# Retention norm: sums by a constant stationary operand, and the factor spread by transfers

## The chip, the cores and the metric

The kernel is one layer of a hybrid encoder on one core of a Trainium2 chip. The metric is the device time of one execution in microseconds (us). A profiled execution gives a trace of every instruction, and a page that sums it up. The engines are TensorE (PE in the rows; its weight loads are PEld), VectorE (DVE), ScalarE (ACT), GpSimd (POOL) and SyncE (SP), which here issues the transfers. SPq in a row is a transfer that SyncE's queue issues.

## The reference

One layer has a combined input projection, eight retention heads and eight windowed attention heads side by side, an output projection, a layer norm, a SwiGLU feed-forward block and a second layer norm. What the change touches is the group norm of the retention heads. Each head has 64 channels, and each position is normalized over them:

```
y = y_f + y_b
mu = jnp.mean(y, axis=-1, keepdims=True)
var = jnp.mean(jnp.square(y - mu), axis=-1, keepdims=True)
y = (y - mu) * lax.rsqrt(var + GN_EPS)
y = ... * gn_gain                       # per channel
return y * jax.nn.silu(gate)
```

Sequence length is 1024, model width 1024, and everything is float32.

## The kernel before, in words

The span has these stages: the first projections (0 to 64 us), the attention of the first pair of heads with more projections (to 120), four retention pairs, each but the first together with an attention pair (to 344), a tail, and from 357.6 on the output projection and the feed-forward block.

**Layout.** A retention pair is two heads. Their output y is held as 128 partitions (2 heads x 64 channels) by 1024 positions, in two halves of 512. The mean is already zero, since the values are centred when they are projected. So the norm needs, for each head and position, the sum of squares over 64 partitions, and the factor (sum / 64 + eps) to the power −1/2 on each of those 64 partitions.

**The norm of a half** has four steps in the class `Retention`. `out` (line 476) makes a 128x512 bank of PSUM called bo. `evict` lets ScalarE write the squares to the buffer rb (line 483) and VectorE copy y (line 484). `norm` has TensorE take each 128x128 block of squares as the stationary operand, with two columns of a constant moving through it (line 490, four matmuls in the code and eight in the trace). The sums come out with positions on the partitions, 128x8. VectorE scales them (line 492), GpSimd raises them to the power −1/2 (line 493), and ScalarE copies each number 64 times (line 495). `turn` has TensorE transpose the four blocks back (line 500), and VectorE multiplies y by the gain and by the factor out of PSUM (line 502).

**Order.** TensorE's order is written out by hand: `run` takes a list of steps in which F stands for a share of the fillers, that is, steps of the remaining projections (`mm3`: three 128x512 matmuls, lines 77 to 79). In the list, K is the keys (transposes, line 404, and VectorE's key evictions, line 407), Y is `out`, E `evict`, M `norm`, X `turn`, Q the retention scores; `sco`, `trn` and `val` are the attention's steps. A pair's second norm and second turn, M(1) and X(1), stand in the list of the next pair, and those of the last pair in a short tail. The other engines' orders are set by a scheduler. Every filler step counts one tick, 48 in a pair's list and 16 in the tail, and the lists `later` and `side` release work when a tick is reached.

**Presplit.** The work in `side` prepares operands for later products: `put` (lines 581 to 584) splits a matrix into a high part (ScalarE, line 582) and a low part (VectorE, line 583) and stores both to DRAM by SyncE (line 584): to pgd and ptd, to wod for the output projection and to ped for a later product. In the last pair, all splits use one buffer called aq. After the last stores SyncE loads the first product's operands from wod (line 794, buffers w and u in turn). TensorE starts the product at lines 783 to 785, and its first sum takes four such operands, w, u, w, u. The transfers of the scan's states stand at line 443, and a small start load with 64 partitions by 8 numbers at line 203.

Of the kernel before, what the change touches and what calls it, by code (L numbers as in the profile page):

```python
# [30 lines left out]
LAG = 3  # L31
NLAG = 7


C_ID, C_DP, C_DN = 0, 128, 256
C_QD, C_BASE = 384, 512
C_KF, C_KB, C_MH, C_TWO, C_BD = 896, 897, 898, 899, 900
C_W = 902

C_MF, C_MB = 902, 1030  # L40


def layer(tc, xT, xn, w_first, w_mt, w_rv, w_out, w_pg, w_pe, pT, w_gu, w_dn,
# [148 lines left out]
    mraw = bt([P, 2, P], "sq", 1)  # L192
    sp.dma_start(mraw, consts[:, C_MF:C_MF + 2 * P].rearrange("p (a b) -> p a b", a=2))
    pool.tensor_copy(masks, mraw)
# [5 lines left out]
    rr = cp.tile([P, 24], F32, name="rr")  # L200
# [3 lines left out]
    lt = cp.tile([P, 4, 24], F32, name="lt")  # L204
# [11 lines left out]
    dve.scalar_tensor_tensor(lg, rr, -1.0, t_, ALU.mult, ALU.mult)  # L216
    kd = cp.tile([P, 2, 8], F32, name="kd")
# [119 lines left out]
    def proj_rv():  # L337
# [12 lines left out]
        def step(t, kt):  # L350
# [5 lines left out]
            if kt == KT - 1:  # L356
                g = b.rearrange("p (g e) -> p g e", e=64)
                sm = bt([P, 3, 8], "sm", 2)
                dve.tensor_reduce(sm[:, 0, :], g, AX.X, ALU.add, negate=True)
                dve.scalar_tensor_tensor(rv[:, t, :].rearrange("p (g e) -> p g e", e=64),  # L360
                                         sm[:, 0, :].unsqueeze(2).to_broadcast([P, 8, 64]), 1.0 / 64, g,
                                         ALU.mult, ALU.add)
# [25 lines left out]
    class Retention:  # L388


        def __init__(self, i, y, states):
            self.i, self.y, self.states = i, y, states
            self.rk, self.dq, _ = pairs[i]
            self.U = [bt([P, NT - 1, 64], f"kv{d}") for d in range(2)]
            self.kdec, self.pt, self.qq, self.r = {}, {}, {}, {}
# [17 lines left out]
        def kv(self):  # L413

            for q in range(2):
# [64 lines left out]
        def evict(self, hh):  # L480
            of = self.o.rearrange("p n c -> p (n c)")
            sq = self.sq = bt([P, HF], "rb")
            act.activation(sq, of, AF.Square)
            dve.tensor_copy(self.half(hh), of)

        def norm(self, hh):

            b = self.o[:, :, 0:2]
            for j in range(4):
                pe.matmul(b[:, j, :], self.sq[:, j * P:(j + 1) * P], cst[:, C_BD:C_BD + 2], start=True, stop=True)  # L490
            sm = bt([P, 3, 8], "sm", 2)
            dve.tensor_scalar(sm[:, 0, :].rearrange("p (n h) -> p n h", h=2), b, 1.0 / 64, EPS, ALU.mult, ALU.add)
            pool.tensor_tensor(sm[:, 1, :], sm[:, 0, :], cst[:, C_MH:C_MH + 1].to_broadcast([P, 8]), ALU.pow)
            r = self.r[hh] = bt([P, 4, 2, 64], "rb")
            act.activation(r.rearrange("p n h e -> p (n h) e"), sm[:, 1, :].unsqueeze(2).to_broadcast([P, 8, 64]), AF.Copy)

        def turn(self, hh):
            tb = bank("to"[hh], (P, 4, P))
            for j in range(4):
                pe.transpose(tb[:, j, :], self.r[hh][:, j].rearrange("p h e -> p (h e)"), ident)  # L500
            y = self.half(hh)
            dve.scalar_tensor_tensor(y, y, gn[:, self.i:self.i + 1], tb.rearrange("p n c -> p (n c)"), ALU.mult, ALU.mult)
# [71 lines left out]
    dr = ent(tc.tile_pool(name="dr", bufs=1, space=bass.MemoryType.DRAM))  # L574
    pgd = dr.tile([7, 4, P, 2, HF], F32, name="pgd")
# [144 lines left out]
    with tc.manual_schedule(engines={mybir.EngineType.PE}):  # L720
# [19 lines left out]
        Q, X = (lambda q: (r.scores, q)), (lambda q: (r.turn, q))  # L740
# [1214 lines left out]
```

## Time and profile before

| what | value |
|---|---|
| median of 3 runs | 1173.65 us (1173.09 to 1173.94) |
| profiled execution | 1172.67 us |
| its span, first to last instruction | 1170.9 us |
| TensorE busy | 1160.2 us (99%) |
| VectorE / ScalarE / GpSimd busy | 892.8 / 580.6 / 120.8 us |
| mean granted TensorE clock | 0.997 |

A row of a timeline has the start in the span, the duration, the engine, the line and operation, the tiles (output<-input) and, in brackets, how long the engine sat idle before it and what ended that. A row of a group of instructions has the minimum, median and maximum duration in ns, and the first and last start. In the chain of work that ended last, each piece is what the next one waited for.

### The profile page before, as it was taken

To read this page: it belongs to the slowest core of one execution; us is meant where nothing else is said; L and a number is where in the kernel's file an instruction comes from. 1 tells how busy PE (TensorE), PEld (TensorE's weight loads), DVE (VectorE), ACT (ScalarE), POOL (GpSimd) and SP (SyncE) were. 2 spreads that over 40 slices of the span, in tenths; PEclk is the share of its full clock that TensorE was granted. 3 is DMA by queue.
4 is the path that set the end of the run, shared out by engine and by line. 5 is a ranking of instruction groups with operands and counts; after the bars stand their busy time and mean duration, and the time that the engine had idled before them with its cause. 6 is when DMAs were issued, how large, how long until landed. Compare 5 with 4: busy or idle time off the path is not lost.

```text
span 1170.9 us, 17982 instructions
## 1 busy us (share of the span) xinstructions
PE 1160.2 (99%) x6410; PEld 978.4 (84%) x6410; DVE 892.8 (76%) x1736; ACT 580.6 (50%) x1181; POOL 120.8 (10%) x181
## 2 busy tenths in 40 slices
PE   9999999999999999999999999999999999999996
PEld 7888888888888888888888888888888888888885
DVE  4566678776859688948998988888888976774677
ACT  5566347776756256214445434443344445552463
POOL 2001020202010021000000000000000011124242
PEclk9999999999999999999999999999999999999998
DMA  7345656546346945756323323332224289999977
GB/s 254 100 152 210 243 193 225 205 134 224 113 157 234 376 170 184 276 185 211 117 90 104 114 103 100 104 131 104 100 72 135 88 249 344 346 236 213 263 161 213
DMA packets 80665, 211.76 MB, mean 181 GB/s; under 512 B 9536, under 2 KB 14784, under 8 KB 80576
## 3 DMA queue, kind: packets, MB, share of 16 engines
q1 hardware_dynamic: 71936, 193.84, 47.5%
q0 software_dynamic: 8640, 16.78, 8.2%
q8 instruction: 50, 0.82, 0.3%
q14 instruction: 39, 0.32, 0.1%
HBM read 139.29 MB, written 62.13 MB: 172 GB/s over the span
## 4 chain that ended last, share of the span: by engine, by line
PE 97%; DVE 1%; DMA 1%; issue 0%; ACT 0%; SPq 0%; DVEq 0%
PE bmm L783 8%; PE bmm L784 8%; PE bmm L785 8%; PE bt L783 6%; PE bt L784 6%; PE bt L785 6%; PE bmm L77 6%; PE bmm L79 6%; PE bmm L78 6%; PE bs L784 4%; PE bs L785 4%; PE bs L783 4%; PE bo L783 4%; PE bo L785 4%; PE bo L784 4%; PE bo L565 2%
## 5 line engine op out<-in xcount | busy, mean ns | idle before, releaser
L77 PE MATMUL bmm<-H,w 128*128 128x512 f32 x240 | 97.2, 405 | 0.3 <-ACT H L71 0.3
L79 PE MATMUL bmm<-H,w 128*128 128x512 f32 x240 | 94.1, 392 | 0.0
L78 PE MATMUL bmm<-H,w 128*128 128x512 f32 x240 | 94.0, 392 | 0.0
L1368 ACT ACTIVATE ev<-ev 128x512 f32<-128x512 f32 x42 | 26.4, 630 | 104.3 <-DVE ev L1397 92.8
L1542 POOL DMA_DIRECT2D h0b<-in_w_dn x24 | 21.6, 900 | 540.7 <-PE bt L785 504.1
L77 PEld LDWEIGHTS bmm<-H,w 128*128 128x128 f32 x240 | 45.1, 188 | 9.9 <-ACT H L71 0.8
L79 PEld LDWEIGHTS bmm<-H,w 128*128 128x128 f32 x240 | 45.0, 188 | 10.0
L78 PEld LDWEIGHTS bmm<-H,w 128*128 128x128 f32 x240 | 45.2, 188 | 8.2 <-DVE H L72 0.4
L535 ACT ACTIVATE sc<-sc,st 128x385 f32<-128x385 f32 (+1 forms) x64 | 37.1, 584 | 16.5 <-DVE st L533 16.4
L531 DVE CUSTOM_DVE_ANT_0 sc<-cst,bs,skb 128x384 f32<-128x384 f32 (+1 forms) x64 | 34.9, 576 | 8.4 <-PE bs L530 7.6
L1397 DVE TENSOR_TENSOR ev<-ev,bt 128x512 f32<-128x512 f32 x44 | 30.1, 683 | 12.5 <-PE bt L785 12.5
L1348 DVE TENSOR_TENSOR ev<-ev,bs 128x256 f32<-128x256 f32 x63 | 25.6, 418 | 15.5 <-PE bs L785 14.7
L1370 DVE TENSOR_TENSOR ev<-ev 128x512 f32<-128x512 f32 x42 | 29.0, 691 | 10.5 <-ACT ev L1368 9.0
L783 PE MATMUL bmm<-H,u 128*128 128x512 f32 x92 | 36.1, 393 | 0.0
L784 PE MATMUL bmm<-H,u 128*128 128x512 f32 x92 | 36.0, 392 | 0.0
L785 PE MATMUL bmm<-H,u 128*128 128x512 f32 x92 | 35.8, 389 | 0.0
L72 DVE TENSOR_TENSOR w<-raw,w 128x512 fp32r<-128x512 f32 x34 | 23.3, 694 | 15.5 <-ACT w L71 15.3
L541 ACT ACTIVATE sc<-sc,st 128x384 f32<-128x384 f32 (+1 forms) x64 | 34.1, 580 | 1.1 <-DVE st L539 1.1
L526 POOL COPY sc<-skb 128x1 f32<-128x1 f32 x64 | 15.6, 252 | 180.1 <-PE bt L553 156.3
L783 PE MATMUL bmm<-H,w 128*128 128x512 f32 x84 | 32.9, 392 | 0.0
L784 PE MATMUL bmm<-H,w 128*128 128x512 f32 x84 | 32.9, 392 | 0.0
L785 PE MATMUL bmm<-H,w 128*128 128x512 f32 x84 | 32.7, 389 | 0.0
(791 smaller groups left out, 3892.6 us busy)
## 6 DMA issues: line engine op xcount, KB each, us to landing
ad<-ev SPq DMA_DIRECT2D x33, 512.0 KB, 2.7
pgd<-pro SPq DMA_DIRECT2D x28, 512.0 KB, 2.9
raw<-in_w_gu SPq DMA_DIRECT2D x22, 512.0 KB, 3.6
ln<-in_w_gu SPq DMA_DIRECT2D x22, 512.0 KB, 4.0
raw<-ad SPq DMA_DIRECT2D x40, 256.0 KB, 6.0
ln<-ad SPq DMA_DIRECT2D x37, 256.0 KB, 6.8
H<-in_w_dn SPq DMA_DIRECT2D x33, 256.0 KB, 7.6
wod<-aq SPq DMA_DIRECT2D x15, 512.0 KB, 2.7
```

Source lines behind the costliest of these rows:

```text
L77: pe.matmul(o, lh, rh, start=start, stop=False)
L78: pe.matmul(o, lh, rl, start=False, stop=False)
L79: recent[0] = pe.matmul(o, ll, rh, start=False, stop=stop).ins.name
L531: dve.tensor_tensor_reduce(sc[g][:, :nk], cst[:, tc0:tc0 + nk], b[:, :nk], slope(i, g), skb[:, 2 * i + g:2 * i + g + 1], ALU.add, ALU.max, ...
L535: act.activation(sc[g][:, :nk + 1], sc[g][:, :nk + 1], AF.Exp, bias=st_[:, 1, j, g:g + 1], accum_out=st_[:, 2, j, g:g + 1])
L541: behind(act.activation(sc[g][:, :nk], sc[g][:, :nk], AF.Copy, scale=st_[:, 3, j, g:g + 1]))
L783: pe.matmul(o, lh, rh, start=start, stop=False, skip_group_check=True)
L784: pe.matmul(o, lh, rl, start=False, stop=False, skip_group_check=True)
L785: pe.matmul(o, ll, rh, start=False, stop=stop, skip_group_check=True)
L1368: act.activation(c[:, 0, :], c[:, 0, :], AF.Silu)
L1370: dve.tensor_tensor(c[:, 1, :], c[:, 0, :], c[:, 1, :], ALU.mult)
L1397: dve.tensor_tensor(get(name), ev[left][:, m, :], right, ALU.add)
```

## The change

The squares become the moving operand. `evict` writes them twice, once in full and once rounded to the matmul's fp32r type, and VectorE forms the difference, so that two parts carry the full precision. `norm` multiplies both with a constant 128x128 matrix called ones as the stationary operand, which adds up in the same bank. Rows 0 and 1 of the result are the sums of the two heads for 512 positions. VectorE scales these two rows, and five steps are put in `later`, at 3, 6, 9, 12 and 15 ticks after the norm: `spread` (two transfers that lay the 2x512 row out over 128 partitions by 8 numbers), `power` (GpSimd, as before on 128x8), `store` (one transfer to DRAM), `fetch` (two transfers that bring each head's 512 numbers back onto 64 partitions) and `scaled` (VectorE's product from on-chip memory). `turn` and its steps in the lists are dropped. The buffers of these steps share names with others (kv0, kv1, qq, pt, rb). To make room, two 128x128 constants go, for which `decay_k` uses a slice of another with a negated factor, and temporaries of the start share buffers.

In the changed code, the norm's matmuls have line 498, the scaled row 500, spread 505, power 508, store 511, fetch 515, the product 519; the key evictions have 411, the presplit stores 604, the loads from wod 814.

On SyncE, at the end of the stage, the queue before stands like this (raw and w are weights, in_w_pe a weight in DRAM):

```order
L584 DMA wod<-aq_3021 128x1024
L597 DMA raw_3660<-in_w_pe 128x1024
L584 DMA ped<-aq_3021 128x1024 x2
L794 DMA w_3812<-wod 128x1024
L584 DMA ped<-aq_3021 128x1024 x2
L794 DMA u_3814<-wod 128x1024
L794 DMA w_3816<-wod 128x1024
```

The loads of u and w stand right behind the last store to ped here. On the same queue, the changed program has this (sn is the 128x8 tile, rnd the place in DRAM, rb the fetched factor):

```order
L617 DMA raw_3679<-in_w_pe 128x1024
L515 DMA kv_3562<-rnd 64x512 x2
L604 DMA ped<-aq_3038 128x1024 x2
L814 DMA w_3833<-wod 128x1024
L604 DMA ped<-aq_3038 128x1024
L505 DMA sn_3757<-kv_3755 64x1x8 x2
L511 DMA rnd<-sn_3757 128x8
L604 DMA ped<-aq_3038 128x1024
L515 DMA rb_3758<-rnd 64x512 x2
L814 DMA u_3835<-wod 128x1024
L814 DMA w_3837<-wod 128x1024
```

The spread and the store now stand between the third and the fourth store to ped, and the fetch between that one and the loads of u, w and u.

On VectorE, ahead of the third pair's key evictions (pro and pre belong to the presplit, qq is the evicted keys), the order before is this:

```order
L643 TENSOR_TENSOR pre_1158<-pre_1159,pre_1158 128x512
L72 TENSOR_TENSOR w_2323<-raw_2321,w_2323 128x512
L643 TENSOR_TENSOR pre_1159<-pre_1159,pre_1158 128x512
L583 TENSOR_TENSOR pro_1162<-pre_1158,pro_1162 128x512
L407 TENSOR_TENSOR qq_2309<-bt_2304,kd 128x512
L247 SCALAR_TENSOR_TENSOR aq_2229<-bmm_2235,aq_2229 64x512
```

The evictions follow on presplit work. At that place the changed program has this:

```order
L663 TENSOR_TENSOR pre_1163<-pre_1164,pre_1163 128x512
L72 TENSOR_TENSOR w_2333<-raw_2331,w_2333 128x512
L663 TENSOR_TENSOR pre_1164<-pre_1164,pre_1163 128x512
L603 TENSOR_TENSOR pro_1167<-pre_1163,pro_1167 128x512
L519 SCALAR_TENSOR_TENSOR y_1590<-y_1590,gn,kv_2113 128x512
L411 TENSOR_TENSOR qq_2322<-bt_2317,kd 128x512
L251 SCALAR_TENSOR_TENSOR aq_2240<-bmm_2246,aq_2240 64x512
```

The product with the fetched factor (line 519, from the buffer kv) now stands directly ahead of the key evictions; its counterpart of before, line 502, stood twelve rows ahead of them.

The diff:

```diff
 LAG = 3
+LAGS = (3, 6, 9, 12, 15)
...
@@ -189,19 +189,21 @@
     cst = cp.tile([P, C_W], F32, name="cst")
     sp.dma_start(cst, consts[:, 0:C_W])
     masks = cp.tile([P, 2, P], mybir.dt.bfloat16, name="masks")
-    mraw = bt([P, 2, P], "sq", 1)
-    sp.dma_start(mraw, consts[:, C_MF:C_MF + 2 * P].rearrange("p (a b) -> p a b", a=2))
-    pool.tensor_copy(masks, mraw)
+    mraw = bt([P, 3, P], "sq", 1)
+    sp.dma_start(mraw, consts[:, C_MF:C_MF + 3 * P].rearrange("p (a b) -> p a b", a=3))
+    pool.tensor_copy(masks, mraw[:, 0:2])
+    ones = cp.tile([P, P], F32R, name="ones")
+    dve.tensor_copy(ones, mraw[:, 2])
     ident = cst[:, C_ID:C_ID + P]
     skb = cp.tile([P, 8], F32, name="skb")
     sp.dma_start(skb, sink.partition_broadcast(P))
     gn = cp.tile([P, 4], F32, name="gn")
     sp.dma_start(gn, gng)
-    rr = cp.tile([P, 24], F32, name="rr")
+    rr = bt([P, 24], "kv0")
     sp.dma_start(rr[:, 0:16], dec_b.partition_broadcast(P))
     for h in range(2):
         sp.dma_start(rr[64 * h:64 * h + 64, 16:24], dec_c[h].partition_broadcast(64))
-    lt = cp.tile([P, 4, 24], F32, name="lt")
+    lt = bt([P, 4, 24], "kv1")
     t_, u_, d_, m_ = (lt[:, i, :] for i in range(4))
     pool.tensor_tensor(t_, cst[:, C_TWO:C_TWO + 1].to_broadcast([P, 24]), rr, ALU.pow)
     dve.tensor_scalar(u_, t_, -1.0, 1.0, ALU.mult, ALU.add)
...
@@ -214,6 +216,8 @@
     dve.tensor_tensor(rr, rr, m_, ALU.mult)
     lg = cp.tile([P, 24], F32, name="lg")
     dve.scalar_tensor_tensor(lg, rr, -1.0, t_, ALU.mult, ALU.mult)
+    nlg = cp.tile([P, 16], F32, name="nlg")
+    dve.tensor_tensor(nlg, rr[:, 0:16], t_[:, 0:16], ALU.mult)
     kd = cp.tile([P, 2, 8], F32, name="kd")
     act.activation(kd[:, 0, :], lg[:, 0:8], AF.Exp, scale=cst[:, C_KF:C_KF + 1])
     act.activation(kd[:, 1, :], lg[:, 8:16], AF.Exp, scale=cst[:, C_KB:C_KB + 1])
...
@@ -374,8 +378,9 @@
 
     def decay_k(i, h):
         e = bt([P, 2, P], "sq", 1)
-        behind(act.activation(e[:, 0, :], cst[:, C_DP:C_DP + P], AF.Exp, scale=lg[:, 2 * i + h:2 * i + h + 1]))
-        behind(act.activation(e[:, 1, :], cst[:, C_DN:C_DN + P], AF.Exp, scale=lg[:, 8 + 2 * i + h:9 + 2 * i + h]))
+        for d in range(2):
+            behind(act.activation(e[:, d, :], cst[:, C_BASE + P:C_BASE + 2 * P], AF.Exp,
+                                  scale=nlg[:, 8 * d + 2 * i + h:8 * d + 2 * i + h + 1]))
         pool.tensor_tensor(e, e, masks, ALU.mult)
         pool.tensor_tensor(decays[i][1][:, h, :], e[:, 0, :], e[:, 1, :], ALU.add)
 
...
@@ -391,8 +396,7 @@
         def __init__(self, i, y, states):
             self.i, self.y, self.states = i, y, states
             self.rk, self.dq, _ = pairs[i]
-            self.U = [bt([P, NT - 1, 64], f"kv{d}") for d in range(2)]
-            self.kdec, self.pt, self.qq, self.r = {}, {}, {}, {}
+            self.kdec, self.pt, self.qq = {}, {}, {}
             self.qd, self.dt = decays[i]
 
         def keys(self, q):
@@ -412,6 +416,7 @@
 
         def kv(self):
 
+            self.U = [bt([P, NT - 1, 64], f"kv{d}") for d in range(2)]
             for q in range(2):
                 b = bank("t", (P, 2, 4, 64))
                 js = [[j for j in range(4) if 4 * q + j != (7, 0)[d]] for d in range(2)]
...
@@ -479,27 +484,41 @@
 
         def evict(self, hh):
             of = self.o.rearrange("p n c -> p (n c)")
-            sq = self.sq = bt([P, HF], "rb")
-            act.activation(sq, of, AF.Square)
+            raw, hi, lo = bt([P, HF], ("kv0", "qq")[hh]), bt([P, HF], ("kv1", "pt")[hh], dt=F32R), bt([P, HF], "rb", dt=F32R)
+            act.activation(raw, of, AF.Square)
+            act.activation(hi, of, AF.Square)
             dve.tensor_copy(self.half(hh), of)
+            dve.tensor_tensor(lo, raw, hi.bitcast(F32), ALU.subtract)
+            self.sq = hi, lo
 
         def norm(self, hh):
 
-            b = self.o[:, :, 0:2]
-            for j in range(4):
-                pe.matmul(b[:, j, :], self.sq[:, j * P:(j + 1) * P], cst[:, C_BD:C_BD + 2], start=True, stop=True)
-            sm = bt([P, 3, 8], "sm", 2)
-            dve.tensor_scalar(sm[:, 0, :].rearrange("p (n h) -> p n h", h=2), b, 1.0 / 64, EPS, ALU.mult, ALU.add)
-            pool.tensor_tensor(sm[:, 1, :], sm[:, 0, :], cst[:, C_MH:C_MH + 1].to_broadcast([P, 8]), ALU.pow)
-            r = self.r[hh] = bt([P, 4, 2, 64], "rb")
-            act.activation(r.rearrange("p n h e -> p (n h) e"), sm[:, 1, :].unsqueeze(2).to_broadcast([P, 8, 64]), AF.Copy)
-
-        def turn(self, hh):
-            tb = bank("to"[hh], (P, 4, P))
-            for j in range(4):
-                pe.transpose(tb[:, j, :], self.r[hh][:, j].rearrange("p h e -> p (h e)"), ident)
-            y = self.half(hh)
-            dve.scalar_tensor_tensor(y, y, gn[:, self.i:self.i + 1], tb.rearrange("p n c -> p (n c)"), ALU.mult, ALU.mult)
+            b = self.o.rearrange("p n c -> p (n c)")
+            for k in range(2):
+                pe.matmul(b, ones, self.sq[k], start=k == 0, stop=k == 1)
+            row = bt([2, HF], "kv0")
+            behind(dve.tensor_scalar(row, b[0:2], 1.0 / 64, EPS, ALU.mult, ALU.add))
+            sm, r, home = bt([P, 2, 8], "sn", 1), bt([P, HF], ("kv1", "rb")[hh]), rnd[2 * self.i + hh]
+
+            def spread():
+                for h in range(2):
+                    sp.dma_start(sm[64 * h:64 * h + 64, 0], row[h:h + 1].rearrange("o (q e) -> o q e", e=8))
+
+            def power():
+                behind(pool.tensor_tensor(sm[:, 1], sm[:, 0], cst[:, C_MH:C_MH + 1].to_broadcast([P, 8]), ALU.pow))
+
+            def store():
+                sp.dma_start(home, sm[:, 1])
+
+            def fetch():
+                for h in range(2):
+                    sp.dma_start(r[64 * h:64 * h + 64], home[64 * h:64 * h + 64].rearrange("q e -> (q e)").partition_broadcast(64))
+
+            def scaled():
+                y = self.half(hh)
+                behind(dve.scalar_tensor_tensor(y, y, gn[:, self.i:self.i + 1], r, ALU.mult, ALU.mult))
+
+            later.extend((ticks[0] + at, f) for at, f in zip(LAGS, (spread, power, store, fetch, scaled)))
 
     def span(n):
         return max(n - 1, 0), min(n + 2, NT)
...
@@ -572,6 +591,7 @@
 
 
     dr = ent(tc.tile_pool(name="dr", bufs=1, space=bass.MemoryType.DRAM))
+    rnd = dr.tile([8, P, 8], F32, name="rnd")
     pgd = dr.tile([7, 4, P, 2, HF], F32, name="pgd")
     ped = dr.tile([2, 2, P, 2, HF], F32, name="ped")
     ptd = dr.tile([4, P, 2, HF], F32, name="ptd")
@@ -737,14 +757,14 @@
         states = state_tile()
         r = Retention(0, y0, states)
         K, M = (lambda q: (r.keys, q)), (lambda q: (r.norm, q))
-        Q, X = (lambda q: (r.scores, q)), (lambda q: (r.turn, q))
+        Q = lambda q: (r.scores, q)
         Y, E = (lambda q: (r.out, q)), (lambda q: (r.evict, q))
         run([K(0), F, K(1), F, F, (r.kv,), Q(0), F, (r.scan,), F, F, F, Y(0), E(0), Q(1),
-             F, M(0), (decay_q, 1), F, (decay_k, 1, 0), Y(1), X(0), E(1), (decay_k, 1, 1), F, F], 48)
+             F, M(0), (decay_q, 1), F, (decay_k, 1, 0), Y(1), E(1), (decay_k, 1, 1), F, F], 48)
         V = []
         for i in range(1, NPAIR):
             assert i == 1 or not side, len(side)
-            M1, X1 = M(1), X(1)
+            M1 = M(1)
             r = Retention(i, ytile(2 * i), states)
             a = Attention(i, ytile(2 * i + 1))
             if i == 2:
@@ -758,12 +778,12 @@
                 side.extend(presplit_small(2, op, 32) + presplit_small(3, op, 40))
             G = [(f, i + 1, *x) for f, x in ((decay_q, ()), (decay_k, (0,)), (decay_k, (1,)))] if i + 1 < NPAIR else \
                 [(lambda: None,)] * 3
-            run([K(0), M1, F, K(1), sco(0), F, *V, (r.kv,), Q(0), F, sco(1), X1, F, trn(0), sco(2), (r.scan,), F, trn(1),
+            run([K(0), M1, F, K(1), sco(0), F, *V, (r.kv,), Q(0), F, sco(1), F, trn(0), sco(2), (r.scan,), F, trn(1),
                  sco(3), F, val(0), val(1), F, trn(2), sco(4), F, trn(3), sco(5), F,
                  Y(0), E(0), val(2), val(3), Q(1), F, G[0], trn(4), sco(6), M(0), F, G[1], trn(5), sco(7), F,
-                 G[2], Y(1), val(4), val(5), X(0), E(1), F, trn(6), F, trn(7), F], 48)
+                 G[2], Y(1), val(4), val(5), E(1), F, trn(6), F, trn(7), F], 48)
             V = [val(6), val(7)]
-        run([*V, M(1), F, X(1), F, F], 16)
+        run([*V, M(1), F, F, F], 16)
 
     bp.close()
 
...
@@ -1824,7 +1844,7 @@
         fa = big16((P, 4, 2, 2, Q))
         halves4 = [(fa[:, k, 0], fa[:, k, 1]) for k in range(4)]
         halves4.append(tuple(ct([P, 2, Q], "sg", 2, F32R) for _ in range(2)))
-        fsum.extend([cst[:, 0:Q], cst[:, Q:2 * Q], cst[:, 2 * Q:3 * Q], ct([P, Q], "fs", 1)])
+        fsum.extend([cst[:, 0:Q], cst[:, Q:2 * Q], *(ct([P, Q], "fs", 2) for _ in range(2))])
         fwide = ct([P, 2, Q], "p", 2)
         fine, more = fine_right(2, halves4[:3]), fine_right(4, halves4[3:])
         fine += more
...
-    c = np.zeros((P, C_MB + P), np.float32)
+    c = np.zeros((P, C_BD + P), np.float32)
-    c[:, C_DP:C_DP + P] = np.maximum(k - s, 0)
-    c[:, C_DN:C_DN + P] = np.maximum(s - k, 0)
-    c[:, C_BD:C_BD + 2] = np.arange(2)[None, :] == (s // 64)
+    c[:, C_BD:C_BD + P] = k == s // 64
```

More of the change, by code (lines that the diff above doesn't have):

```diff
@@ L31 @@
 LAG = 3
+LAGS = (3, 6, 9, 12, 15)
 NLAG = 7
[L35 to L40, printed above, removed]
+C_ID, C_QD, C_BASE = 0, 128, 256
+C_KF, C_KB, C_MH, C_TWO = 640, 641, 642, 643
+C_W = 644
+C_MF, C_MB, C_BD = 644, 772, 900
 def layer(tc, xT, xn, w_first, w_mt, w_rv, w_out, w_pg, w_pe, pT, w_gu, w_dn,
@@ L486, in norm @@
         def norm(self, hh):
-            b = self.o[:, :, 0:2]
-            for j in range(4):
[L490 to L493, printed above, removed]
-            r = self.r[hh] = bt([P, 4, 2, 64], "rb")
```

5 lines of the change are left out of this document (3 added, 2 removed).

## The prediction

> **What bounds the kernel now.** I read the engine shares first, then the chain of work that ended last, then the windows of the attention and retention stage, and last the chain and the timelines around the places that the change touches. A measurement of this kernel can tell a change from none at about 0.2%, which is 2.35 us.
>
> ```profile
> PE 1160.2 (99%) x6410; PEld 978.4 (84%) x6410; DVE 892.8 (76%) x1736; ACT 580.6 (50%) x1181; POOL 120.8 (10%) x181
> ...
> PE 97%; DVE 1%; DMA 1%; issue 0%; ACT 0%; SPq 0%; DVEq 0%
> ...
> 163.90:223.70 59.80, 59.67 (x475) 50.67 (x474) 47.20 (x117) 44.61 (x106) 10.44 (x22) 1.00 0.56 193
> ```
>
> TensorE is busy for 99% of the span and makes up 97% of the chain, so a matmul saved is time saved unless something makes TensorE wait. The third row is a window with the second of the four retention pairs. Its columns are the window, its length, the busy time of TensorE, weight loads, VectorE, ScalarE and GpSimd, the granted clock, the DMA share and GB/s. VectorE has 12.6 of 59.8 us free there, ScalarE 15.2, and the clock is full.
>
> TensorE's only wait inside the stage's reach is at its end, where the output projection takes over. This is the chain there (start, duration, what):
>
> ```profile
> 345.34 0.98 PE bo L490 x8
> ...
> 349.85 0.45 PE bo L500 x4
> 350.36 0.63 issue
> 350.99 0.70 DVE aq L583
> 351.70 0.32 SPq L584
> 352.07 0.43 SPq L794
> 352.59 0.73 SPq L794
> 353.37 6.46 DMA u<-wod
> 359.97 0.47 PE bt L783
> ```
>
> The last presplit store goes out at 351.70. Behind it, on the same queue, come the three loads for the first product, at 352.07, 352.59 and 353.37. The last of them lands at 359.83, and TensorE resumes with it at 359.97. It had to wait 0.15 us only, because fillers kept it busy until 357.6. So two paths are level here, TensorE's own work and the queue's, and a gain on one alone is not a gain.
>
> **What TensorE saves.** These are its rows around a norm, a turn, and the last norm and turn:
>
> ```profile
> 150.74 0.39 PE L79 MATMUL bmm<-H,w 128*128 128x512 f32 x1
> 150.97 0.95 PE L490 MATMUL bo<-cst,rb 128*128 128x2 f32 x8
> 151.78 0.48 PE L77 MATMUL bmm<-H,w 128*128 128x512 f32 x1
> 152.09 0.39 PE L78 MATMUL bmm<-H,w 128*128 128x512 f32 x1
> 152.32 0.39 PE L79 MATMUL bmm<-H,w 128*128 128x512 f32 x1
> ...
> 157.26 0.66 PE L500 MATMUL bt<-cst,rb 128*128 128x128 f32 x4
> 157.67 0.48 PE L77 MATMUL bmm<-H,w 128*128 128x512 f32 x1
> ...
> 345.27 1.05 PE L490 MATMUL bo<-cst,rb 128*128 128x2 f32 x8
> 346.19 0.48 PE L77 MATMUL bmm<-H,w 128*128 128x512 f32 x1
> ...
> 349.68 0.60 PE L500 MATMUL bo<-cst,rb 128*128 128x128 f32 x4
> 350.04 0.47 PE L77 MATMUL bmm<-H,w 128*128 128x512 f32 x1
> 350.35 0.39 PE L78 MATMUL bmm<-H,w 128*128 128x512 f32 x1
> ```
>
> A 128x512 matmul follows another after 0.23 us. The norm of line 490 holds TensorE for 151.78 − 150.97 = 0.81 us, and the next step is 0.31 instead of 0.23, so it costs 0.89. A turn (line 500) takes 350.35 − 349.68 − 0.23 = 0.44, or 0.41 at 157.26. With two norms of 0.81 to 0.89 and two turns of 0.41 to 0.44, a pair loses about 2.56 us. It gets four 128x512 matmuls instead, 4 x 0.23 = 0.91. The balance is −1.65 us a pair, −6.6 for four. By the start of the last norm it is −5.8: the last turn's 0.44 and the last norm's 0.4 come later.
>
> **What the other engines get.** Median durations of the operations removed, and the price of those added:
>
> ```profile
> L483 ACT ACTIVATE rb<-bo x8: 574/591/599, 147.1 to 336.1; 128x512 f32<-128x512 f32 x8
> ...
> L484 DVE COPY y<-bo x8: 678/684/692, 148.3 to 336.8; 128x512 f32<-128x512 f32 x8
> ...
> L492 DVE TENSOR_SCALAR sm<-bo x8: 152/164/167, 152.5 to 346.4; 128x8 f32<-128x8 f32 x8
> ...
> L493 POOL TENSOR_TENSOR sm<-sm,cst x8: 1633/1810/2143, 152.8 to 346.6; 128x8 f32<-128x8 f32 x8
> ...
> L495 ACT ACTIVATE rb<-sm x8: 612/628/631, 154.8 to 348.7; 128x512 f32<-128x512 f32 x8
> ...
> L583 DVE TENSOR_TENSOR aq<-raw,aq x11: 684/691/693, 66.6 to 351.0; 128x512 fp32r<-128x512 f32 x11
> ```
>
> ScalarE gains a second Square (0.59) and loses the broadcast copy of line 495 (0.63): nothing. VectorE gets the subtraction for the low part, 0.69 as in line 583, and in place of 0.16 for line 492 a row of 2x512, for which no row stands; it lies between that 0.16 and the 0.68 of a 512-wide copy, and I take 0.65, since the width is the same. That makes +1.2 us a half, 9.5 in all. The product with the factor has the same size as before. Over the path the 9.5 us could cost anything from 0 to 9.5; the free 12.6 us in the window above against 2.4 added puts it near 0. I take 1.0 in all, for the stretches where VectorE or ScalarE runs without a gap: the copy of y waits for two Squares instead of one, and the low part comes behind it.
>
> The six GpSimd and transfer steps are new on their path. These are the nearest transfers, with what each takes from issue to landing:
>
> ```profile
> L443 SPq DMA_DIRECT2D states<-kv x16: 462/552/2181, 139.2 to 304.4; - x16
> ...
> DMA to landing us min/median/max: 2.1/2.3/4.7
> ```
> ```profile
> L203 SPq DMA_DIRECT2D rr<-in_dec_c x2: 487/526/566, 18.3 to 19.6; - x2
> ...
> DMA to landing us min/median/max: 3.7/4.2/4.7
> ```
>
> The first moves whole rows between on-chip buffers in this stage. The second has the spread's own destination shape, 64 partitions by 8 numbers, but comes from DRAM, among the start's loads. I take 2.3 for each leg, because of time and place, and keep 4.2 for the range.
>
> A half then needs, from the end of its matmuls: the row 0.65, the spread 0.5 + 2.3 (two issues), the power 1.8, the store 0.35 + 2.3, and the fetch 1.0 + 2.3. That is 11.2 us, against the 15 ticks (about 1.25 us each, 48 in the 60 us of a run) after which VectorE is told to use it. The place where this is tight is the first half of a pair, because VectorE's queue has the product just ahead of the next pair's key evictions:
>
> ```profile
> 207.01 0.17 DVE L492 TENSOR_SCALAR sm<-bo 128x8 f32<-128x8 f32 x1
> ...
> 224.21 0.69 DVE L407 TENSOR_TENSOR qq<-bt,kd 128x512 f32<-128x512 f32 x1 [0.40 <-PE bt L404]
> ```
>
> The factor would be there at 207.0 + 11.2 = 218.2. The evictions start at 224.2 now, about 2.5 earlier by then, and need the 0.75 of the product before them: slack 2.7 us. So the middle of the stage holds if the legs are on average no more than 0.9 us longer than I take them.
>
> The queue of SyncE issues everything in order, so forty new transfers put their own waits in front of the others: the store waits for the power, the fetch for the store's landing, and behind them stand presplit stores, weight loads, and at the end the three loads above. That is the largest term.
>
> **The end of the stage.** The other rows for it:
>
> ```profile
> 344.10 0.63 ACT L582 ACTIVATE aq<-raw 128x512 fp32r<-128x512 f32 x1 [2.28 <-DMA ped<-aq]
> ...
> 345.49 6.53 SPq L584 DMA_DIRECT2D ped<-aq  x2
> ```
>
> The presplit runs through one buffer: a split waits until the store before it has landed. The third store goes out at 345.49, the fourth at 351.70. In the changed order the spread follows the third, the norm's store comes ahead of the fourth, and the fetch ahead of the three loads. On the old clock axis: the last norm's matmuls start at 345.3 − 5.8 + 1.0 = 340.5 and end at 341.0. The row stands on VectorE behind the third presplit (about 341.5 by the same shift) and is done at 342.2. The spread has landed at 345.0, the power is done at 347.0 (2.01 us at this place), the store has landed at 349.5, and the two fetch issues end at 350.5. The three loads then go out by 351.8, as closely spaced as now (1.3 us). With 5.9 to 6.5 us for the last the operand is there at 357.7 to 358.3, or 357.3 if the fourth presplit store, now 2.7 us ahead of the loads, no longer shares their time. I take 357.7 against 359.97: a gain of 2.3. TensorE itself would be ready at 359.8 − 6.6 + 1.0 = 354.2, so it waits some 3.5 us. Of 6.6 us, 1.0 goes to stalls and 3.3 to the queue. The early constants and the extra temporaries lie at a place where loads and not VectorE are late; I cost them at nothing.
>
> The sum goes from the profiled execution, 1172.67 (span 1170.9 and 1.8 around it) to 1170.4. The median of the runs is 1.0 above the profiled one, so 1173.65 becomes 1171.3.
>
> The Trainium skill, in "DMA: Bandwidth & Descriptors" (Anatomy of one DMA), puts a fixed time of about 2.0 us on a transfer, mostly for the receipt of the write, and says that a wait for a semaphore is done by the issuing sequencer. The 2.1 us minimum above agrees with the first, and the 6.53 us row of two stores with the second; with 2.0 a leg the end would come 0.6 us earlier by estimate.
>
> **Rivals.** *All of it is kept*: the legs are quick and the loads land no later than TensorE is ready, so that −6.6 + 1.0 holds: 1168.1. Against it stands the chain of the row, three transfers and the power, which are all new there.
>
> *Eaten at the end*: the spread alone takes L203's 3.7 to 4.2 (small pieces), which delays the loads by 1.4 to 1.9: 1172.7 to 1173.2; if the presplit pipe also loses a slot (2 us behind a waiting store), 1175.
>
> *Slower, VectorE held by the factor*: if each leg is longer by d, a first half is late by 3d − 2.7, three times, and the end by 2d. The balance is −2.3 + 3(3d − 2.7) + 2d = 11d − 10.4, above zero from d = 0.95 and over 2.35 from 1.16, which is 3.5 us a leg. With L203's shortest, 3.7 (d = 1.4), it gives +5.0, 1178.7. For it speak L203's times and the largest of L443, 4.7; against it L443's median in the very stage.
>
> By the Trainium skill, "DMA: Bandwidth & Descriptors" (Specifications), transfers in pieces under 512 bytes are read, modified and written; the spread writes pieces of 32 bytes, so the page speaks for these last two. No row here shows such a piece between on-chip buffers.
>
> **How the numbers follow.** The forecast, a gain of 1 to 3.5 us (1170.2 to 1172.6), has 0.40, as much above the bound of 2.35 as below. All kept has 0.17, eaten (1172.6 to 1176) 0.17, slower 0.26. That makes faster 0.37, same 0.37, slower 0.26. The range goes from all kept, 1168.1, to just short of the priced slow case, 1178.
>
> **What would show it.** Right: line 490's and 500's groups gone, TensorE's time in a pair 1.6 us shorter, 59.8 to about 58.2; the spread, store and fetch landing in 2.1 to 2.9; in the chain at the end a row, spread, power, store and fetch, and a TensorE gap of 2 to 4 us before the first product. Wrong: idle time of VectorE before the product with the factor or of TensorE ahead of line 411's evictions inside the stage, legs over 3.3 us, or SyncE's waits for the power and the store pushing presplit stores far past their places.

## The result, and the profile after

The changed kernel takes 1176.34 us (median of 20 runs, 1173.95 to 1178.34), against 1173.70 for the kernel before on the same chip. The ratio is 1.0023 with a 95% interval of 1.0016 to 1.0030: slower by 2.6 us, just over the 0.2% bound. The forecast was a gain of 2.3.

From the page of the changed kernel, the engines' row and the chain by engine:

```profile
PE 1157.9 (99%) x6330; PEld 971.8 (83%) x6330; DVE 900.5 (77%) x1746; ACT 580.6 (49%) x1181; POOL 120.1 (10%) x181
...
PE 81%; DVE 7%; ACT 5%; DMA 4%; issue 2%; SPq 0%; POOL 0%; DVEq 0%; ACTq 0%; POOLq 0%
```

TensorE is still busy for 99%, but it makes up only 81% of the chain, against 97% before. VectorE, ScalarE and transfers have come onto the path. TensorE's waits from 60 to 400 us, where the same view of the kernel before lists none, are these (who waited for whom, total, times, longest):

```profile
PE bt L803 <- DMA u<-wod: 3.2, 2, 2.9
PE bt L572 <- ACT ptr L574: 0.8, 1, 0.8
PE bt L428 <- DVE pt L411: 0.7, 1, 0.7
PE bt L572 <- ACT sc L560: 0.4, 1, 0.4
PE bt L803 <- DMA w<-wod: 0.3, 1, 0.3
PE bo L584 <- ACT ptr L574: 0.2, 1, 0.2
```

To see what each place gives and takes I matched the 1056 filler matmuls of TensorE in two timelines by their number, and took the difference of their starts (changed minus before). It moves at each norm and turn (a gain), and wherever TensorE is held (a loss). "Last norm" is the filler behind it; "first product" is the first matmul of line 803, "fourth operand" the one with that operand:

| place | changed, first profile | changed, second profile |
|---|---|---|
| at the 16th filler, ahead of all changed code | +0.78 | +0.40 |
| sum of the gains behind it | −5.8 | −5.6 |
| sum of the losses in the stage | +3.6 | +2.5 |
| last norm | −0.87 | −2.16 |
| first product | −1.41 | −2.70 |
| fourth operand | +2.49 | +1.21 |
| last matmul of the product lines in the kernel | +4.04 | +2.41 |

The second profile is that of the control run below, the changed kernel again. Two things repeat: TensorE is ahead at the first product in both, and has lost 3.9 us by the fourth operand. That the two agree so well is in part chance, as the control run shows. Of the 1.5 us that the first profile loses behind it, 1.2 go at 535 us, at a wait of 0.9 for VectorE that the second profile doesn't have.

This is the end of the stage in the chain of the first profile; it answers to the chain that the prediction shows:

```profile
346.74 0.68 DVE y L724
347.42 0.60 DVE kv L500
348.04 0.48 SPq L505
348.57 1.78 DMA sn<-kv
350.50 1.85 POOL sn L508
352.37 1.39 DMA rnd<-sn
353.81 0.46 SPq L515
354.33 0.58 SPq L515
354.96 0.58 SPq L814
355.58 0.43 SPq L814
356.06 6.27 DMA u<-wod
362.46 0.47 PE bt L803
```

From the row (line 500) to the loads the steps stand as forecast, one behind the other: spread, power, store, fetch, then the loads of u, w and u. But the row is done at 348.0 instead of 342.2, 5.8 us later than forecast, and the last load goes out at 356.06 where it went out at 353.37 before.

The transfers themselves come near the price that was taken for them (2.3 a leg): 1.9 for the spread, 2.3 for the store, 3.0 for the fetch. These are the spread, the store and the fetch of the changed kernel, each with its landing row:

```profile
L505 SPq DMA_DIRECT2D sn<-kv x16: 475/588/605, 157.6 to 348.6; - x16
...
DMA to landing us min/median/max: 1.7/1.9/4.5
```
```profile
L511 SPq DMA_DIRECT2D rnd<-sn x8: 319/326/377, 163.9 to 352.4; - x8
...
DMA to landing us min/median/max: 1.4/2.3/3.2
```
```profile
L515 SPq DMA_DIRECT2D rb<-rnd x8: 461/522/590, 174.5 to 354.3; - x8
...
DMA to landing us min/median/max: 2.8/3.0/4.4
```

The spread's 32-byte pieces land in 1.9 us, faster than the 2.3 of the larger state transfers. So the rule on pieces under 512 bytes, in the Trainium skill's "DMA: Bandwidth & Descriptors" (Specifications), set no price that shows here, and did not bear out the two rivals beside which the prediction cites it.

### The profile page after: what moved, and what is told of

It is laid out like the page before. It is cut to its first block, busy times and chain, and to the rows that moved or that the text cites. A ratio compares the mean times of both kernels' runs of the same rounds, so it can differ in the third digit from the quotient of the medians.

```text
span 1174.9 us, 17927 instructions
## 1 busy us (share of the span) xinstructions
PE 1157.9 (99%) x6330; PEld 971.8 (83%) x6330; DVE 900.5 (77%) x1746; ACT 580.6 (49%) x1181; POOL 120.1 (10%) x181
## 4 chain that ended last, share of the span: by engine, by line
PE 81%; DVE 7%; ACT 5%; DMA 4%; issue 2%; SPq 0%; POOL 0%; DVEq 0%; ACTq 0%; POOLq 0%
PE bmm L803 8%; PE bmm L804 7%; PE bmm L805 7%; PE bt L803 6%; PE bt L804 6%; PE bt L805 6%; PE bs L805 4%; PE bs L804 4%; PE bs L803 4%; PE bo L805 3%; PE bo L803 3%; PE bo L804 3%; PE bmm L77 3%; PE bmm L78 3%; PE bmm L79 3%
## 5 line engine op out<-in xcount | busy, mean ns | idle before, releaser
L77 PE MATMUL bmm<-H,w 128*128 128x512 f32 x240 | 96.9, 404 | 0.0
L78 PE MATMUL bmm<-H,w 128*128 128x512 f32 x240 | 94.1, 392 | 0.0
L79 PE MATMUL bmm<-H,w 128*128 128x512 f32 x240 | 93.8, 391 | 0.0
L1368 DVE TENSOR_TENSOR ev<-ev,bs 128x256 f32<-128x256 f32 x63 | 25.6, 418 | 15.5 <-PE bs L805 14.7
L71 ACT ACTIVATE H<-ln 128x512 fp32r<-128x512 f32 (+1 forms) x34 | 22.7, 676 | 23.0 <-DVE ln L1052 7.2
L545 POOL COPY sc<-skb 128x1 f32<-128x1 f32 x64 | 15.5, 252 | 180.6 <-PE bt L572 141.9
L803 PE MATMUL bmm<-H,w 128*128 128x512 f32 x84 | 32.9, 392 | 0.0
L804 PE MATMUL bmm<-H,w 128*128 128x512 f32 x84 | 32.9, 392 | 0.0
```

What stands on the lines that cost most here:

```text
L77: pe.matmul(o, lh, rh, start=start, stop=False)
L78: pe.matmul(o, lh, rl, start=False, stop=False)
L79: recent[0] = pe.matmul(o, ll, rh, start=False, stop=stop).ins.name
L803: pe.matmul(o, lh, rh, start=start, stop=False, skip_group_check=True)
L804: pe.matmul(o, lh, rl, start=False, stop=False, skip_group_check=True)
```

## The experiments

Where a ratio is given, it is to the kernel before on the same chip, with its 95% interval.

### The last half in the old way

```diff
+def old(i, hh):
+    return i == NPAIR - 1 and hh == 1
...
     def norm(self, hh):
+        if not old(self.i, hh): return self.norm_new(hh)     # evict likewise
+        (four narrow matmuls, line 492 to 495 and the turn of the kernel before)
-        run([*V, M(1), F, F, F], 16)
+        run([*V, M(1), F, X(1), F, F], 16)
```

> Only the very last half (second half of the fourth pair) is done in the old way, with four narrow matmuls, the broadcast copy and a turn in the tail; the other seven halves keep the transfers. Theory A (the price lies in two places: about 2.5 us at the end, where the loads of the first product stand behind the last half's store and fetch, and about 3.5 us in the stage, where VectorE and ScalarE hold TensorE): the loads follow the last presplit store again, the first product's fourth operand comes back to about 360, and the time falls by 1.5 to 3 from the changed kernel's 1176.3, to 1173.3 to 1174.8. Rival B (the waits of SyncE's queue at all eight halves are the price): seven eighths stay, 1175.5 or more.

Measured 1172.18 (11 runs), ratio 0.9987 (0.9979 to 0.9996). One half of eight in the old way takes off 4 us, and the kernel now takes 0.13% less than before: the interval leaves out 1, but the difference is below the 0.2% bound. The time falls by more than theory A had put there, and rival B falls. SyncE's queue and TensorE's fourth operand in this run:

```profile
345.41 5.47 SPq L638 DMA_DIRECT2D ped<-aq  x2
350.93 0.43 SPq L848 DMA_DIRECT2D u<-wod  x1
351.46 0.66 SPq L848 DMA_DIRECT2D w<-wod  x1
352.16 0.48 SPq L848 DMA_DIRECT2D u<-wod  x1
```
```profile
358.31 0.39 PE L839 MATMUL bt<-w,H 128*128 128x512 f32 x1
358.64 0.47 PE L837 MATMUL bt<-u,H 128*128 128x512 f32 x1
```

The third load goes out at 352.16 instead of 356.06, right behind the last presplit store, and the fourth operand holds TensorE no longer than 0.1 us.

### The last half's transfers on GpSimd's queue

```diff
+            q = pool if self.i == NPAIR - 1 and hh == 1 else sp
-                sp.dma_start(...)      # spread, store, fetch
+                q.dma_start(...)
```

> The last half's spread, store and fetch are issued from GpSimd's queue; all else as in the changed kernel. Theory A: if the loads lose time only because they stand behind these transfers on SyncE, they go out with the last presplit store at about 351, and 1.5 to 3 us come back: 1173.3 to 1174.8. Rival C (the end is late because the presplit stores themselves are late, or because the product with the factor is late): less than 1 us comes back, 1175.5 or more.

Measured 1181.14 (5 runs), ratio 1.0066 (1.0053 to 1.0078). The time lies where rival C put it, but the trace has another course. The loads do go out early (the third at 351.59), the first product starts at 354.92 and its fourth operand is used at 357.88, 4.6 us ahead of the changed kernel. So what stood in front of the loads was what made them late. But now the factor is late. The transfers' medians from issue to landing from 335 to 372 us, VectorE's product, and TensorE's wait that follows:

```profile
rb<-rnd POOLq DMA_DIRECT2D x2, 128.0 KB, 5.8
sn<-kv POOLq DMA_DIRECT2D x2, 2.0 KB, 1.8
rnd<-sn POOLq DMA_DIRECT2D x1, 4.0 KB, 5.6
```
```profile
364.35 0.75 DVE L521 SCALAR_TENSOR_TENSOR y<-y,gn,rb 128x512 f32<-128x512 f32 x1 [8.94 <-DMA rb<-rnd]
```
```profile
PE bt L805 <- ACT h0b L974: 7.1, 1, 7.1
```

A store of 4 KB takes 5.6 us and the fetch 5.8 while the loads run. Whether it is the queue or the loads beside it that makes them slow is not separated here. TensorE then waits 7.1 us in the second product, whose operand is a sum that contains this y; the changed kernel has no such wait. So the factor and the loads are needed at nearly the same time: behind the factor's transfers the loads were late, and beside the loads the factor is.

### No transfers

```diff
-            row = bt([2, HF], "kv0")
-            behind(dve.tensor_scalar(row, b[0:2], 1.0 / 64, EPS, ALU.mult, ALU.add))
+            row = bt([P, HF], ("kv1", "rb")[hh])
+            behind(dve.tensor_scalar(row, b, 1.0 / 64, EPS, ALU.mult, ALU.add))
...
-            later.extend(... zip(LAGS, (spread, power, store, fetch, scaled)))
+            later.append((ticks[0] + LAGS[-1], scaled))     # multiplies by row
```

> The two wide matmuls, both squares, the low part and the product stay; spread, power, store and fetch are left out, and the product takes the scaled sums themselves, so the output isn't normalized. VectorE's scaling is of 128x512 instead of 2x512. Theory A: the end's loss goes, and the stage's stalls stay since VectorE and ScalarE have the same work: TensorE keeps about 1 to 2 us, 1171.5 to 1173. Rival B: without transfers nothing holds TensorE, and its whole saving of 5 to 6 us is kept, 1168 to 1169.

Measured 1169.39 (5 runs), ratio 0.9964 (0.9950 to 0.9977): 4 us faster than before, 7 faster than the changed kernel. Neither expectation has it: the saving of TensorE is there (−5.9 in the matched fillers), 1.6 us of it is lost in the stage, and nothing at the end. So the transfers, with GpSimd's step between them, cost 7 us in all, and the loss that is there without them is not far from the 1.0 of the prediction.

### No low part

```diff
-            act.activation(raw, of, AF.Square)
             act.activation(hi, of, AF.Square)
-            dve.tensor_tensor(lo, raw, hi.bitcast(F32), ALU.subtract)
...
-            for k in range(2):
-                pe.matmul(b, ones, self.sq[k], start=k == 0, stop=k == 1)
+            pe.matmul(b, ones, self.sq, start=True, stop=True)
```

> The low part is left out: one square and one wide matmul a half, so the sums have only the reduced precision of the rounded part. ScalarE loses eight squares (4.7 us), VectorE eight subtractions (5.5), TensorE eight matmuls (1.8); all transfers stay. Theory A: the stage's stalls fall to near 0, TensorE reaches the last norm 4 us or more earlier, and some of that is taken by the transfers at the end: 1172.5 to 1174.5. Rival B: the transfers' waits stay as they are, only TensorE's 1.8 goes: 1174.5 to 1176.

Measured 1174.50 (11 runs), ratio 1.0006 (0.9998 to 1.0015). It is the upper end of theory A's range and the lower end of B's. The trace decides: the stage's losses did not fall, they are 3.4 us, though ScalarE and VectorE have 10 us less to do. TensorE saves 8.1 and is 4.1 ahead at the first product, and 2.8 of that goes in a wait for u. So taking away the second square and the subtraction does not take away the stage's stalls.

### All second halves in the old way

The condition is `hh == 1`, otherwise as in the first experiment.

> All four second halves are done in the old way, the four first halves with transfers. Theory A' (formed from the runs before: the last half's transfers cost about 4 us at the end; in the stage the transfers and the added work of ScalarE and VectorE take back about a third of what TensorE saves, evenly over the halves): TensorE saves 0.85 x 4 = 3.4 less about 1.2, with no loss at the end: 1171 to 1172.3, so no worse than the run with only the last half old (1172.2). Rival D (the first halves are the dear ones, since their product stands ahead of the next pair's key evictions): 1172.8 or more.

Measured 1173.26 (11 runs), ratio 1.0001 (0.9992 to 1.0010), outside what A' gave and on the side of D. With transfers the three second halves inside the stage seem to gain 1.1 us rather than to cost (the first experiment has them, at 1172.18; the two intervals overlap a little), so they are not the dear ones. But the trace shows other places than D named: 0.8 us is lost at one wait for ScalarE late in the second pair, 1.1 at the last turn, which waits 0.9 for its factor, and nothing at the third pair's key evictions, although the first halves' products still stand there. So D is not shown.

### The old way, with the splits' work added

```diff
+            act.activation(hi, of, AF.Square)
             dve.tensor_copy(self.half(hh), of)
+            dve.tensor_tensor(lo, sq, hi.bitcast(F32), ALU.subtract)
```

> All halves in the old way (narrow matmuls, copy, turns, no transfers), with the second square and the subtraction for the low part added, whose results are not used. TensorE has its old work. Theory E (the added work of ScalarE and VectorE itself stalls the stage): 1.5 us or more above before, 1175.2 or more. Theory F (with TensorE at its old pace the added work is hidden; the stalls of the changed kernel come only as TensorE runs ahead of a chain on VectorE and ScalarE that was nearly as late before): within 0.7 us of before, 1173.0 to 1174.4.

Measured 1174.63 (11 runs), ratio 1.0010 (1.0001 to 1.0019), between the two. All halves are old here. The trace has the stage unchanged to 0.1 us up to 264 us, which is theory F, and then one wait, for the scores' decay product in the third pair (line 466 here). These are TensorE's rows there:

```profile
266.32 0.44 PE L585 MATMUL bs<-k,aq 128*128 128x384 f32 x1 [0.69 <-DVE pt L466]
...
269.34 0.63 PE L83 MATMUL bmm<-H,w 128*128 128x512 f32 x1
269.77 0.63 PE L84 MATMUL bmm<-H,w 128*128 128x512 f32 x1
```

From 269 on the matmuls follow one another after 0.43 instead of 0.23 us, for 3.5 us. The granted clock is 0.62 in the window from 268 to 272. So 1.2 us were lost at a wait of 0.7, and 1.7 more by the clock behind it. That the wait set off the clock's fall is not shown: the first profile of the changed kernel has waits of 0.7 and 0.8 in the stage without one.

### The changed kernel again

> The changed kernel unchanged, for a second profile: how much of the late start (0.8 us by the eighth filler) and of the waits in the stage is its own and how much differs from execution to execution. If the stalls are the same, the fillers' lead at the last turn's place is 1.4 us again and the span 1173 to 1176; the median 1175.5 to 1177.

Measured 1175.63 (11 runs), ratio 1.0019 (1.0010 to 1.0028). The late start is half as long, 0.40, and in other runs it lies between −0.36 and 0.90, so it differs from execution to execution; the code there is the same in all these runs. The stalls stand at the same places but are shorter (2.5 us). Behind the wait for u this execution has what the first didn't. The windows there, with the granted clock in the third column from the end:

```profile
358.00:360.00 2.00, 1.86 (x4) 1.11 (x5) 2.00 (x4) 0.00 (x0) 0.00 (x0) 0.50 1.02 408
360.00:362.00 2.00, 2.00 (x5) 1.42 (x6) 2.00 (x5) 0.49 (x1) 0.00 (x0) 0.50 1.02 416
362.00:364.00 2.00, 2.00 (x6) 1.58 (x5) 2.00 (x5) 1.98 (x5) 0.00 (x0) 0.50 1.02 418
364.00:366.00 2.00, 2.00 (x8) 1.55 (x8) 2.00 (x4) 1.99 (x4) 0.00 (x0) 0.84 0.43 166
```

TensorE waits 2.3 us and then runs at half its clock for 6 us. Between the first matmul with u and the end of that stretch the difference to before goes from −0.2 to +2.7. Of this, 1.4 lies ahead of the fourth operand, where the first profile, at full clock, loses 0.8 in waits for the loads; 1.5 lies behind it. So here the half clock, and not a load, sets the start of the fourth operand (no wait for it is listed).

### The last pair in the old way

The condition is `i == NPAIR - 1`.

> Both halves of the fourth pair in the old way. If the first half's fetch, which stands ahead of the presplit stores, matters beyond the last half's transfers, the loads go out 2 us earlier than with only the last half old, and the time is 1171.5 or less. If TensorE alone decides there, it only loses that half's 0.8 us: 1172.6 to 1173.2.

Measured 1172.40 (11 runs), ratio 0.9995 (0.9986 to 1.0003). It lies between the two expectations, and the difference to the first experiment, 0.2, is not resolved. So the first half's fetch costs nothing that is resolved here once the last half is old. What it does in the changed kernel, where the loads wait for the last half, this run can't show.

### Matmuls in the wait

```diff
+        def pad():
+            b = bank("o")
+            for _ in range(12):
+                pe.matmul(b, ones, xs[0][:, 0, 0:HF], start=True, stop=True)
-        run([*V, M(1), F, F, F], 16)
+        run([*V, M(1), F, F, F, (pad,)], 16)
```

> The changed kernel with twelve matmuls (128x512, 2.7 us) whose result is not used, put ahead of the first product, where TensorE waited 2.3 and 2.9 us in the two profiles of it. Theory G (that wait is dear twice: in one of the two profiles and in the run without the low part the granted clock falls to 0.5 for 5 to 7 us after it, which costs another 2 us or so): no long wait, the clock stays at 1.00 after it, and the time falls by 1 to 2 us, to 1173.8 to 1175.0, although TensorE has more to do. Rival H (the drop of the clock is chance and has no part in the median): the matmuls fill the wait and change nothing, 1175.6 to 1176.5.

Measured 1176.07 (11 runs), ratio 1.0024 (1.0015 to 1.0033): no change, as rival H has it. The mean granted clock of these runs is 0.9976 against 0.9968 in the control run, so the clock is kept; and in the profile no wait at this place is longer than 0.4 us. But the time is not lower. TensorE, busy with these matmuls until the loads come, gains nothing: the loss at the end is the late loads, and the clock is at most a part that can't be had back in this way.

### No low part, and the last half in the old way

> The last half in the old way, and the other seven without the low part (one square, one wide matmul; the sums of squares have the rounded part's precision only). If the gains add up: 1172.2 of the run with the last half old, less 1.6 for seven matmuls, 1170.3 to 1171.2. If TensorE, further ahead, only meets the chain of VectorE and ScalarE earlier: 1171.5 to 1172.2.

Measured 1172.05 (11 runs), ratio 0.9988 (0.9979 to 0.9997): the gains don't add up. Without the loss at the end, seven matmuls less (1.6 us) are worth 0.1. In the trace the stage's losses up to the last turn grow to 5 us. So TensorE, further ahead, waits for VectorE and ScalarE, which is the second expectation.

### All halves in the old way

> All eight halves in the old way inside the changed kernel: the constants, the temporaries of the start and the shared buffers as changed. A control on these: if they cost nothing, as the prediction has it, 1173.0 to 1174.2; if the start's 0.1 to 0.9 us is theirs, 1174.2 or more.

Measured 1173.28 (11 runs), ratio 0.9998 (0.9989 to 1.0007). The constants, the temporaries and the buffers cost nothing that shows. Against this run, the one with the splits' work added (ratio 1.0010) is 0.12% longer, though the intervals touch: that work seems to cost about 1.4 us even with TensorE at its old pace.

## Why the prediction was wrong

**What TensorE saves** held. Where they can be told from a loss beside them, the turns gave 0.38 to 0.45 a piece for the 0.41 to 0.44 worked out, the norms 0.40 to 0.44 where 0.81 to 0.89 less 0.46 had been expected. The sums in the table, 5.6 to 5.8 for 6.6, are smaller because at three places a gain and a loss fall on the same step and only the rest is seen; the stage's losses are then larger than the table's by as much.

**The stalls of the stage** is the first step that failed. They were put at 1.0 and are at least 3.6 and 2.5 in the two profiles. Of this, 1.6 is there without transfers. The prediction took TensorE's empty list of waits, and VectorE's 12.6 free us in 60, as slack. But the chain of the kernel before, in the second pair, already left TensorE. These are its longest pieces just ahead of the attention's transposes (line 553, line 572 after):

```profile
178.36 0.66 DVE y L502
...
179.66 0.79 ACT sc L535 x3
...
180.87 1.08 ACT sc L541 x2
...
182.41 0.37 ACT ptr L555
...
182.82 0.87 PE bt L553 x6
```

TensorE waited 0.0 us there because it arrived as the softmax was ready, not because the softmax had time. Whatever TensorE gains ahead of such a join is lost in it. In the changed kernel this join is where the wait of 0.8 for line 574 stands. That the low part's removal left the losses at 3.4, and was worth 0.1 once the end was mended, shows the same. Some of the losses are new: at the third pair's key evictions, VectorE has the product (line 519) ahead of them, where line 502 did not stand, and a row of 0.68 us (line 500) where line 492 took 0.17, and TensorE waits 0.7. Before and after:

```profile
227.70 0.17 DVE L492 TENSOR_SCALAR sm<-bo 128x8 f32<-128x8 f32 x1
...
228.50 1.28 DVE L407 TENSOR_TENSOR pt<-bt,kd 128x512 f32<-128x512 f32 x2
```
```profile
225.15 0.74 DVE L519 SCALAR_TENSOR_TENSOR y<-y,gn,kv 128x512 f32<-128x512 f32 x1
...
229.41 0.68 DVE L500 TENSOR_SCALAR kv<-bo 2x512 f32<-2x512 f32 x1
...
230.73 1.28 DVE L411 TENSOR_TENSOR pt<-bt,kd 128x512 f32<-128x512 f32 x2
```

The product alone does not do it: with the second halves in the old way it still stands there, the row does not, and nothing is lost at this place. How the rest is shared between the transfers' places in SyncE's queue, which hold the presplit, and the added work of VectorE and ScalarE is not settled: without transfers 1.6 of losses remain, with them 2.5 and 3.6 in two executions of one kernel.

**The row** was sized right (0.65 taken, 0.67 measured), and so were the legs on average (2.4 for 2.3; the fetch took 3.0). The slower rival, VectorE held by the factor with legs of 3.5 us or more, did not happen: VectorE waited for a factor once, at the very end.

**The end of the stage** is the second step that failed, and it decides the time. The mechanism was right, loads held back by the last half's store and fetch, and so was the length of the chain: from the end of the row to the fourth operand 15.5 us were forecast, and 14.4 were measured in the first profile (14.6 in the second, where the half clock sets the last of it). What was wrong is where the chain starts. The row was to be done at 342.2 and was done at 348.0 and 346.6.

The last norm was to start at 340.5 and started at 344.7 and 343.5. That is the stage's stalls again and, for 0.8 and 0.4, the start. Then the row was held until 347.3 and 345.9 by the third presplit and line 724, which stand ahead of it on VectorE. These are the second profile's rows of SyncE and VectorE:

```profile
334.90 1.10 SPq L515 DMA_DIRECT2D kv<-rnd  x2
336.06 5.38 SPq L604 DMA_DIRECT2D ped<-aq  x2
```
```profile
344.70 0.69 DVE L603 TENSOR_TENSOR aq<-raw,aq 128x512 fp32r<-128x512 f32 x1 [1.06 <-ACT aq L602]
345.31 0.68 DVE L724 SCALAR_TENSOR_TENSOR y<-sq,y 128x512 f32<-128x512 f32 x1
345.92 0.67 DVE L500 TENSOR_SCALAR kv<-bo 2x512 f32<-2x512 f32 x1
```

The prediction had moved the presplit earlier by as much as TensorE. It did not come earlier: the third split's low part started at 344.8 before and at 346.1 and 344.7 in the changed kernel. Its splits wait for the landing of each store before, and two of these stores now have the factor's transfers ahead of them: the first went out 2.1 to 2.3 us after its split was done, behind the first half's fetch, and the fourth stands behind the last half's store. The prediction had named such a lost slot of the presplit pipe in a rival, but not in its sum.

So the fourth operand came at 362.5 and 361.2 instead of 357.7. This term was to give back 3.3 us and gave back 3.9 from a smaller lead. Behind it the second profile lost 1.5 more at half the clock. That the last half's transfers are the cause at the end, the undoing of this half alone shows: it is worth 4 us in the median.

**The rivals.** The likeliest was a gain of 1 to 3.5. What came is nearest to "eaten at the end", which had 0.17: on the prediction's scale the loss of 2.6 gives 1176.3, just past that rival's 1176. Its slow spread did not happen (1.9 us), its lost slot of the presplit did, and one cause was not in it: most of TensorE's lead at the last norm was never there. By its sign the result belongs to "slower", which had 0.26 for a mechanism that did not occur.

**The best version** is that with the last half in the old way, 1172.18, or the same without the low part, 1172.05: both 0.12 to 0.13% below the kernel before, less than the 0.2% bound, and not to be told apart.

## What to carry to other kernels

An engine that never waits may still have no slack: look in the chain for pieces of other engines just ahead of it, for there a saving is lost. Count a saving only up to the next such join, and shift the work of other queues by their own pace, not by that of the engine that got faster. A latency of ten us can cost little in the middle of a steady stage, where VectorE never waited for a factor, and is dear in its last step, where other transfers are queued behind it: the change no longer cost time when its last instance was left out.

## What was not expected of the hardware

The granted clock of TensorE fell to 0.5 to 0.6 for 3.5 to 6 us behind waits of 0.7 us (the old way with the splits' work), 2.3 (the changed kernel again), 2.8 (no low part) and 7.1 (GpSimd's queue), and did not behind a wait of 2.9 in the first profile of the changed kernel. The Trainium skill, in "TensorE: Matmul & The Clock Gate" (Part 1), has the clock fall after an idle window of about 3.4 us; here it fell behind shorter waits as well. Two transfers issued from GpSimd's queue, the store of 4 KB and the fetch, took 5.6 and 5.8 us while SyncE's loads ran at 328 GB/s from 352 to 356 us and at 417 from 356 to 360; on SyncE's queue the same store took 2.3.
